# A hybrid backbone step: gates and half a modulation summed on VectorE from transposed weights, the state-space task run two groups at once, VectorE work moved to ScalarE

## The chip, the cores and the metric

The kernel runs on one core of a Trainium2 chip. The metric is the device time of one execution in microseconds (us), the median of three runs. The names of the trace are PE for TensorE's matmuls, PEld for its weight loads, DVE for VectorE, ACT for ScalarE, POOL for GpSimd and SP for the queue that issues most DMAs.

## The reference, cut to what matters

Two layers act on 384 tokens (128 context, 256 latent) of width 2048, all in float32.

```
mod = silu(c) @ w_ada + b_ada              # w_ada: 2048 x 6144; c for latent, c_ctx for context tokens
shift, scale, gate = split(mod, 3)         # 2048 columns each
u = LN(x) * (1 + scale) + shift
proj = u @ w_in                            # 2048 x 6160, feeds four mixers:
#   windowed attention, a state-space scan, pooling, neighbourhood attention
x = LN_affine(alpha * x + gate * (concat(silu(gate_g) * mixer_g) @ w_out))
```

So each layer needs two vectors (context, latent) times a 2048 x 6144 matrix, and two large products, u @ w_in and the mixers' output @ w_out.

## The kernel before, in words

The weights stream from DRAM once. A float32 weight tile of 128 x 1024 (`raw`) is split into a high part `whi` on ScalarE (`split_hi`, L1289) and the rest `wlo` on VectorE (`split_lo`, L1293), up to `HL_BUFS` = 4 items ahead of TensorE, and the activations are split likewise into `uhi` and `ulo`. Every product is three matmuls (`tok_mm` L1399, `t_mm` L1406). `CHUNKS` cuts the 6160 columns of w_in into 13 chunks; w_out follows in three groups of 512 columns (`cc` 0 to 2) and two of 256. Five PSUM banks take these products and are emptied by `evac` (L1018) and `wo_evac` (L1124); three serve all else (`mbank`).

The order on each engine is fixed when the program is built. `slots` (L1201 to L1250) lists the weight items; between two of them `advance` (L400) runs a step of a background task (attention units, convolutions, `gen_B`, `gen_Bs` and `gen_Bi` of the state space, pooling) where the clocks of `Plan` (L152) say that it is ready and that the work booked on VectorE and ScalarE ends at most `SLACK` us after TensorE's. `Plan` books a VectorE operation with two SBUF inputs and a GpSimd operation one after the other. `finish` forces tasks to their end where their results are needed; `finish_B` does so for the state space before the chunk `gd` is evacuated, because its output lies in the part of `mx` that `gd` writes.

The modulation (`ada_items` L1203) is computed on TensorE. A step is 512 columns of w_ada; its eight items, of two 128 x 512 weight tiles each, go in two bursts of four: `ada_mm` (L455) multiplies with the two vectors in four column strips of 32, `ada_evac` adds the strips up in `part`. For shift and scale `mod_mm` (L474) sums the four strips with `sel2` by four small matmuls and `mod_evac` adds the bias. For a gate (steps 8 to 11) `gen_gate` (L498) gathers the strips by one matmul with 512 columns, adds the bias, writes the row to DRAM (`gscr`) and reads it back on all 128 partitions. Layer 0's shift and scale are made at the start, beside its first three chunks. Layer 1's steps 0, 4, 1, 5, 2, 6 stand between layer 0's other chunks, its steps 3 and 7 in the layer boundary (`boundary`, L1416), and the gate steps of each layer in chunk `gc` and in cc 0 to 2.

`copy` (L337) alternates between ScalarE and VectorE where no engine is named. `unit` (L546) is one attention unit: scores, `tensor_tensor_reduce` for the maximum, exponential, and a scaling of the probabilities on VectorE.

Of the kernel before, what the change touches and what calls it, by code (L numbers as in the profile page):

```python
# [34 lines left out]
ARENA = 14600  # L35
# [3 lines left out]
HL_BUFS = 4  # L39

# [111 lines left out]
class Plan:  # L152
# [11 lines left out]
    def region(self, ap):  # L164
# [11 lines left out]
        if len(dims) > 1 and dims[0][1] <= 4:  # L176
# [6 lines left out]
              "arena", "bank")  # L183
# [25 lines left out]
    def cost(self, e, name, out, kw):  # L209
        src = kw.get("in_", kw.get("in0", out))  # L210
        n = max(math.prod(a.shape[1:]) for a in (out, src))
        if e == "PE":
            if name == "transpose":
                return 0.11
            wide = kw["rhs"].dtype == F32R
            c = 0.0105 + n * 0.00043 if wide else max(0.003 + n * 0.001675, 0.222)
            return c * 0.25 if kw.get("tile_position") is not None else c
        if e == "V":
            fast = name in ("tensor_copy", "tensor_scalar", "memset") and not src.tensor.name.startswith("bank")
            return 0.065 * (1 + hasattr(kw.get("scalar1"), "tensor")) + n * (0.00053 if fast else 0.00105)  # L220
        if e == "S":
            return 0.1 + n * 0.00083 + (0.18 if kw.get("accum_out") is not None else 0.0)
# [7 lines left out]
    def charge(self, e, name, args, kw):  # L230
# [3 lines left out]
               if hasattr(a, "tensor")]  # L234
        if e == "S" and args[2] in (AF.Exp, AF.Silu) and args[2] != self.table:
# [23 lines left out]
class Eng:  # L259
    def __init__(self, eng, key, plan):  # L260
        self.eng, self.key, self.plan = eng, key, plan

    def __getattr__(self, name):
        f = getattr(self.eng, name)

        def call(*a, **k):
            self.plan.charge(self.key, name, a, k)
# [5 lines left out]
def hybrid_step(ctx: ExitStack, tc: tile.TileContext,  # L273
                x_prompt, x_sample, cache_attn_k, cache_attn_v, cache_na_k, cache_na_v,
                state_f, state_b, c, c_ctx, w_ada, b_ada, w_in, w_out, ln_g, ln_b,
# [22 lines left out]
    bT = sb.tile([P, DEPTH, 2, KT], F32, name="bT")  # L298
# [19 lines left out]
    gscr = [dr.tile([4, 2, 512], F32, name=f"gscr{i}") for i in range(DEPTH)]  # L318
# [48 lines left out]
    WINDOW = 6  # L367
    BLOCKED = object()
    SLACK = 1.0
# [85 lines left out]
    def ada_mm(its):  # L455
        half = its[0]["i"] // 4
        bk = mbank()
        for g in range(2):
            for j in range(4):
                r = its[2 * g + j // 2]["raw"]  # L460
                PE.matmul(bk[32 * j:32 * j + 32, :], lhsT=scT[:, 8 * half + 4 * g + j, :],
                          rhs=r[:, (j % 2) * 512:(j % 2) * 512 + 512], start=g == 0, stop=g == 1,
# [3 lines left out]
    def ada_evac(its, bk):  # L466
        half = its[0]["i"] // 4
        if half == 0:
# [3 lines left out]
        return half == 1  # L472

    def mod_mm():  # L474
        bk = mbank()
        for b in range(4):
            PE.matmul(bk[:, 2 * b:2 * b + 2], lhsT=part[:, b * 128:b * 128 + 128], rhs=sel2, start=True, stop=True)
        return bk

    def mod_evac(l, step, bk):  # L480
# [4 lines left out]
        V.tensor_tensor(out=mod[:, l, w:w + nw, k:k + nk, :],  # L485
# [1322 lines left out]
```

## Time and profile before

| | us |
|---|---|
| median of 3 runs (1396.72 to 1399.25) | 1397.04 |
| the profiled execution, its own time | 1397.24 |
| its span, first to last instruction | 1395.5 |
| TensorE busy in it | 1342.4 |
| VectorE / ScalarE / GpSimd busy | 752.8 / 461.4 / 175.9 |

The span is the time between the first and the last instruction of the one execution that was profiled. Busy time is a union: two matmul records that overlap count once, and the end of a matmul is modelled. Start times in the trace are microseconds from the span's start.

### The profile page before, as it was taken

What the parts mean: (1) busy time and instruction counts of PE and PEld (TensorE: products, weight loads), DVE (VectorE), ACT (ScalarE), POOL (GpSimd) and SP (SyncE); (2) the same over time, 40 slices, a digit from 0 to 9 for tenths busy, and PEclk for the clock granted to TensorE, in tenths of its full rate; (3) what the DMA queues carried; (4) which work ended last, traced back from release to release, by engine and by line L of the source; (5) the groups of instructions that cost most, each with busy time, mean ns of one, the idle gap of its engine ahead of it and who ended that gap; (6) DMA issues with size and microseconds to landing.
All of it is one profiled execution on the core that took longest, in us unless ns stands there. A gap on an engine that the chain in (4) does not pass through costs nothing.

```text
span 1395.5 us, 19994 instructions
## 1 busy us (share of the span) xinstructions
PE 1342.4 (96%) x7769; PEld 1148.2 (82%) x7769; DVE 752.8 (54%) x1262; ACT 461.4 (33%) x709; POOL 175.9 (13%) x290
## 2 busy tenths in 40 slices
PE   5999999999999999999988999999999999999995
PEld 2776798899987999867786689999999899977785
DVE  4444555676574445554467344566456544554447
ACT  1222343332323243422228524333322343242220
POOL 1111110003430114000000000000234011300000
PEclk9999999999999999999998999999999999999998
DMA  9999764457675733777867544334555654577772
GB/s 328 357 357 301 243 190 152 139 167 260 206 252 185 247 103 109 258 249 244 274 201 248 174 134 118 91 110 120 146 150 166 170 154 115 163 246 258 265 233 96
DMA packets 179446, 278.29 MB, mean 199 GB/s; under 512 B 19688, under 2 KB 78968, under 8 KB 178456
## 3 DMA queue, kind: packets, MB, share of 16 engines
q1 hardware_dynamic: 176248, 269.07, 59.9%
q0 software_dynamic: 2240, 6.38, 1.6%
q10 hardware_dynamic: 864, 1.57, 0.3%
q8 instruction: 61, 1.00, 0.3%
q14 instruction: 33, 0.27, 0.1%
HBM read 267.98 MB, written 10.83 MB: 200 GB/s over the span
## 4 chain that ended last, share of the span: by engine, by line
PE 80%; DVE 6%; DMA 6%; issue 4%; ACT 3%; POOL 0%; SPq 0%; DVEq 0%; ACTq 0%; POOLq 0%
PE bank L268 80%; DVE arena L268 3%; DVE mx L268 2%; DMA rawa<-in_w_ada_dram 2%; DMA gscr<-arena 1%; ACT whi L268 1%; DVE wlo L268 1%; DMA arena<-gscr 1%; ACT arena L268 1%; DMA cst<-in_tables_dram 1%; DMA arena<-in_w_ada_dram 1%; ACT ucat L268 1%; DMA raw<-in_w_in_dram 0%; ACT uhi L268 0%; ACT L268 0%
## 5 line engine op out<-in xcount | busy, mean ns | idle before, releaser
L268 DVE TENSOR_TENSOR wlo<-raw,whi 128x1024 fp32r<-128x1024 f32 (+1 forms) x248 | 318.9, 1290 | 316.8 <-ACT whi L268 313.1
L268 ACT ACTIVATE whi<-raw 128x1024 fp32r<-128x1024 f32 (+1 forms) x256 | 269.4, 1058 | 400.6 <-PE bank L268 280.9
L268 PE MATMUL bank<-uhi,whi 128*128 128x384 f32 x1024 | 368.5, 360 | 4.3 <-ACT mx L268 2.7
L268 PE MATMUL bank<-whi,uhi 128*128 128x512 f32 (+2 forms) x960 | 344.8, 359 | 5.5 <-ACT uhi L268 4.0
L268 PE MATMUL bank<-uhi,wlo 128*128 128x384 f32 x1024 | 344.8, 337 | 0.0
L268 PE MATMUL bank<-ulo,whi 128*128 128x384 f32 x1024 | 344.5, 336 | 0.0
L268 PE MATMUL bank<-wlo,uhi 128*128 128x512 f32 (+2 forms) x960 | 337.8, 352 | 1.9 <-POOL wlo L268 1.9
L268 PE MATMUL bank<-whi,ulo 128*128 128x512 f32 (+2 forms) x960 | 338.2, 352 | 0.2 <-DVE ulo L268 0.2
L268 PEld LDWEIGHTS bank<-whi,uhi 128*128 128x128 f32 x960 | 183.1, 191 | 57.1 <-issue 14.5
L268 PEld LDWEIGHTS bank<-uhi,whi 128*128 128x128 f32 x1024 | 192.7, 188 | 21.2 <-issue 5.9
L268 PEld LDWEIGHTS bank<-wlo,uhi 128*128 128x128 f32 x960 | 183.3, 191 | 25.6 <-POOL wlo L268 2.6
L268 PEld LDWEIGHTS bank<-whi,ulo 128*128 128x128 f32 x960 | 182.6, 190 | 26.1 <-DVE ulo L268 1.1
L268 PEld LDWEIGHTS bank<-ulo,whi 128*128 128x128 f32 x1024 | 192.9, 188 | 5.8
L268 PEld LDWEIGHTS bank<-uhi,wlo 128*128 128x128 f32 x1024 | 192.2, 188 | 0.0
L268 ACT ACTIVATE arena<-arena 128x384 f32<-128x384 f32 (+7 forms) x85 | 44.1, 523 | 207.9 <-DVE arena L268 206.8
L268 PE MATMUL bank<-arena 128*128 128x128 f32 (+3 forms) x440 | 88.0, 325 | 0.1
L268 PE MATMUL bank<-rawa,scT 128*32 128x512 f32 x608 | 77.9, 604 | 8.1 <-DMA rawa<-in_w_ada_dram 8.1
L268 POOL TENSOR_TENSOR arena<-arena 128x512 f32<-128x512 f32 (+4 forms) x60 | 70.3, 1188 | 67.0 <-DVE arena L268 57.6
L268 ACT ACTIVATE arena<-bank 128x384 f32<-128x384 f32 (+2 forms) x92 | 39.0, 439 | 85.3 <-PE bank L268 82.9
L268 PEld LDWEIGHTS bank<-arena 128*128 128x128 f32 x440 | 64.4, 190 | 1.3 <-DVE arena L268 0.3
L268 PE MATMUL bank<-cst,arena 128*128 128x128 f32 (+1 forms) x273 | 45.6, 278 | 14.7 <-ACT arena L268 6.6
L268 PEld LDWEIGHTS bank<-rawa,scT 128*32 128x32 f32 x608 | 17.4, 109 | 47.3 <-issue 41.0
(83 smaller groups left out, 849.4 us busy)
## 6 DMA issues: line engine op xcount, KB each, us to landing
raw<-in_w_in_dram SPq DMA_DIRECT2D x176, 512.0 KB
rawa<-in_w_ada_dram SPq DMA_DIRECT2D x128, 512.0 KB
raw<-in_w_out_dram SPq DMA_DIRECT2D x64, 512.0 KB
arena<-in_w_ada_dram SPq DMA_DIRECT2D x80, 256.0 KB
rawa<-in_w_ada_dram SPq DMA_DIRECT2D x48, 256.0 KB
raw<-in_w_in_dram SPq DMA_DIRECT2D x16, 528.0 KB
arena<-lscr POOLq DMA_DIRECT2D x24, 256.0 KB, 4.6
arena<-gscr SPq DMA_DIRECT2D x8, 512.0 KB
```

What stands on the lines that cost most here:

```text
L268: return f(*a, **k)
```

## The change

- The gates of both layers, and steps 0, 4, 1, 5 of layer 1's shift and scale, are no longer made on TensorE. The host hands w_ada transposed as well (`w_adat`: a column of w_ada lies along a row). A tile holds 128 columns of w_ada on the partitions and 1024 of its 2048 rows; VectorE multiplies it by `silu(c)`, which is replicated on all partitions in `scb` (1 MB per half of the rows, read from the small DRAM tensor `csc`), and sums along the row with `tensor_tensor_reduce`, once for the context and once for the latent vector. `vq` lists 96 such tiles: 32 for layer 0's gate, 32 for layer 1's half of shift and scale, 32 for layer 1's gate. They lie in the four `rawa` buffers, and while w_out of layer 0 runs in two buffers of the arena.
- The reductions are placed by the planner: `v_fill` after each group of matmuls where VectorE's clock is behind TensorE's and the tile has landed, `v_hole` before a VectorE operation that would wait 0.6 us or more, and `v_until` where results are needed.
- A gate is finished by one transpose and one DRAM round trip per layer instead of four.
- `mod_mm` transposes the strips, and VectorE adds them up (`tensor_reduce`) in `mod_evac`.
- `gen_Bi` waits for and computes the decay of two groups ahead of the matmuls; its output has its own buffer `bo` in the arena, `finish_B` is gone, and the three norms are tasks of their own.
- From VectorE to ScalarE: modulation in `u_prep`, scaling in `unit`, the first tap of `gen_conv`, and `copy` gives ScalarE three of four.
- In the boundary `xn` has half its size (its second half is written after four transposes read the first), and `ucat` has four slots instead of three. `SLACK` is 2.0. Layer 1's steps 2 and 6 move to layer 0's cc 1 and 2. Some of `Plan`'s costs are changed, and the scratch for GpSimd's DMA descriptors is given as 4096 bytes.

```diff
+RAW_V = 2
+V_STEPS = (0, 4, 1, 5)
...
+    gcol = sb.tile([P, 2, KT], F32, name="gcol")
+    vpart = sb.tile([P, 32, 2], F32, name="vpart")
+    scb = sb.tile([P, 2, 1024], F32, name="scb")
-    ucat = sb.tile([P, 2, T], F32, name="ucat")
+    ucat = sb.tile([P, 2, 512], F32, name="ucat")
...
-            flip[0] ^= 1
-            eng = "S" if flip[0] else "V"
+            flip[0] = (flip[0] + 1) % 4
+            eng = "V" if flip[0] == 0 else "S"
...
+    V_HOLE = 0.6
-    SLACK = 1.0
+    SLACK = 2.0
...
-        V.tensor_tensor(out=mod[:, l, w:w + nw, k:k + nk, :],
-                        in0=bk[:, 0:8].rearrange("p (w k v) -> p w k v", w=nw, k=nk),
+        m = vsum[:, :, :]
+        V.tensor_reduce(out=m, in_=bk.rearrange("p (b j v) -> p b v j", b=4, j=4)[:, :, 0:2, :],
+                        axis=mybir.AxisListType.X, op=OP.add)
+        V.tensor_tensor(out=mod[:, l, w:w + nw, k:k + nk, :], in0=m.rearrange("p (w k) v -> p w k v", w=nw),
...
-            PE.matmul(bk[:, 2 * b:2 * b + 2], lhsT=part[:, b * 128:b * 128 + 128], rhs=sel2, start=True, stop=True)
+            PE.transpose(bk[:, b * 128:b * 128 + 128], part[:, b * 128:b * 128 + 128], ident)
...
-    def gen_gate(l, step):
-        cc = step - 8
+    def gen_gate(l, cc):
+        if cc == 0:
+            gt = yield from get(128)
+            bk = mbank()
+            PE.transpose(bk[0:32, 0:128], gcol[:, :, :].rearrange("p v k -> p (v k)"), ident)
+            copy(gt.v()[0:32, :], bk[0:32, 0:128], "S")
+            dma(nc.sync, gscr[l].rearrange("v (k p) -> (v k) p", p=P), gt.v()[0:32, :])
+            yield
+            gt.free()
-        src = bass.AP(tensor=b_ada.tensor, offset=b_ada.offset + l * 6144 + step * 512, ap=[[0, 2], [1, 512]])
-        dma(nc.gpsimd, gb.v(512, 1024)[0:2, :], src)
-        bk = mbank()
-        PE.matmul(bk[0:2, :], lhsT=sel2, rhs=part[:, :], start=True, stop=True)
-        V.tensor_tensor(out=gb.v(0, 512)[0:2, :], in0=bk[0:2, :], in1=gb.v(512, 1024)[0:2, :], op=OP.add)
-        dma(nc.sync, gscr[l][cc], gb.v(0, 512)[0:2, :])
-        yield
-        src = bass.AP(tensor=gscr[l].tensor, offset=gscr[l].offset + cc * 1024, ap=[[0, P], [1, 1024]])
-        dma(nc.sync, gb.v(), src)
+        src = bass.AP(tensor=gscr[l].tensor, offset=gscr[l].offset + cc * 512, ap=[[0, P], [D, 2], [1, 512]])
+        dma(nc.sync, gb.m(2, 512), src)
+    vq = []
+    vq += [dict(l=0, w=2, kt=j, half=h) for h in (0, 1) for j in range(KT)]
+    vq += [dict(l=1, w=s_ // 4, kt=4 * (s_ % 4) + j, half=h) for h in (1, 0) for s_ in V_STEPS for j in range(4)]
+    vq += [dict(l=1, w=2, kt=j, half=h) for h in (0, 1) for j in range(KT)]
+    vload, vdone = [0], [0]
+    vseen = {}
+    vhalf = [None]
+    vring = [rawa, []]
+    def v_load():
+        ring = vring[0]
+        while vload[0] < min(vlimit[0], vdone[0] + len(ring)):
+            it = vq[vload[0]]
+            c0 = it["w"] * D + it["kt"] * P
+            it["raw"] = ring[vload[0] % len(ring)]
+            dma(nc.sync, it["raw"][:, :], w_adat[it["l"], c0:c0 + P, it["half"] * 1024:it["half"] * 1024 + 1024])
+            vload[0] += 1
...
+    def v_half(h):
+        if vhalf[0] != h:
+            vhalf[0] = h
+            dma(nc.sync, scb[:, :, :], bass.AP(tensor=csc.tensor, offset=csc.offset + h * 1024,
+                                               ap=[[0, P], [D, 2], [1, 1024]]))
+    def v_step(more=True):
+        it = vq[vdone[0]]
+        v = it.setdefault("v", 0)
+        v_half(it["half"])
+        key = (it["l"], it["w"], it["kt"])
+        first = it["half"] == vfirst[it["l"], it["w"]]
+        if first and v == 0:
+            vseen[key] = vdone[0] % 32
+        slot = vseen[key]
+        init = bT[:, it["l"], it["w"], it["kt"]:it["kt"] + 1] if first else vpart[:, slot, v:v + 1]
+        if first:
+            dst = vpart[:, slot, v:v + 1]
+        elif it["w"] == 2:
+            dst = gcol[:, v, it["kt"]:it["kt"] + 1]
+        else:
+            dst = modcol(it["l"], it["kt"], it["w"], v)
+        V.before = None
+        V.tensor_tensor_reduce(out=uflat[:, :] if v == 0 else it["raw"][:, :], in0=it["raw"][:, :], in1=scb[:, v, :],
+                               scale=1.0, scalar=init, op0=OP.mult, op1=OP.add, accum_out=dst)
+        V.before = v_hole
+        it["v"] = v + 1
+        if v == 1:
+            vdone[0] += 1
+            if more:
+                v_load()
+            if vdone[0] < len(vq):
+                v_half(vq[vdone[0]]["half"])
+    def v_ready():
+        if vdone[0] >= vlimit[0] or vload[0] <= vdone[0]:
+            return 1e9
+        return max(plan.ready([], [vq[vdone[0]]["raw"], scb[:, :, :]]), clk["V"])
+    def v_hole(t):
+        while t - clk["V"] >= V_HOLE and v_ready() <= clk["V"] + 0.1:
+            v_step()
+    vlimit = [0]
+    vfirst = {(0, 2): 0, (1, 0): 1, (1, 1): 1, (1, 2): 0}
+    V_GATE = {0: 32, 1: 96}
+    V_ALL = {0: 64, 1: 96}
+    def v_until(n, more=True):
+        while vdone[0] < n:
+            v_step(more)
+    def v_fill():
+        while v_ready() <= clk["PE"]:
+            v_step()
...
-        u = ucat[:, kt % 2, :]
-        V.tensor_scalar(out=u[:, 0:128], in0=bk[:, 0:128], scalar1=modcol(l, kt, 1, 0),
-                        scalar2=modcol(l, kt, 0, 0), op0=OP.mult, op1=OP.add)
-        V.tensor_scalar(out=u[:, 128:384], in0=bk[:, 128:384], scalar1=modcol(l, kt, 1, 1),
-                        scalar2=modcol(l, kt, 0, 1), op0=OP.mult, op1=OP.add)
+        u = ucat[:, kt % 2, 0:T]
+        S.activation(u[:, 0:128], bk[:, 0:128], AF.Identity, bias=modcol(l, kt, 0, 0), scale=modcol(l, kt, 1, 0))
+        S.activation(u[:, 128:384], bk[:, 128:384], AF.Identity, bias=modcol(l, kt, 0, 1), scale=modcol(l, kt, 1, 1))
...
-        V.tensor_scalar(out=sc.v(0, nk), in0=sc.v(0, nk), scalar1=st[:, 2:3], scalar2=None, op0=OP.mult)
+        S.activation(sc.v(0, nk), sc.v(0, nk), AF.Copy, scale=st[:, 2:3])
...
-        V.tensor_scalar(out=o, in0=xp.v(0, 388), scalar1=w[0], scalar2=b, op0=OP.mult, op1=OP.add)
+        S.activation(o, xp.v(0, 388), AF.Identity, bias=b, scale=w[0])
...
-        return mx[:, 12 * T + 512 * t:12 * T + 512 * t + 512]
+        return lay[l]["bo"].v(512 * t, 512 * t + 512)
+        d["bo"] = yield from get(1536)
...
-        yield lr.v()
+        yield lr.v(0, 1024)
+        decay(0)
+        cb(1)
+        yield lr.v(1024, 2048)
+        decay(1)
+        yield
-            decay(i)
-            if i % 2 == 0 and t < 2:
-                cb(t + 1)
-            yield
+                if i == 1:
+                    cb(2)
+                yield lr.v(1024 * (i % 2), 1024 * (i % 2) + 1024)
+                decay(i + 2)
...
+        def norm(t):
+        for t in range(3):
+            spawn(norm(t), ("Bn", l, t), True)
...
-            if name == "gd":
-                finish_B(l)
...
-        o, x = lay[l]["xn"].v(2048 * t + c0, 2048 * t + c0 + n), mxX[:, t, c0:c0 + n]
+        o, x = lay[l]["xn"].v(1024 * t + c0 % 1024, 1024 * t + c0 % 1024 + n), mxX[:, t, c0:c0 + n]
...
-            for s in (0, 4, 1, 5, 2, 6):
+            for s in (2, 6):
-        gside = ada_items(l, 8)
-        for m in main:
-            slots.append(m)
-            if CHUNKS[m["ch"]][0] == "gc":
-                slots.append(gside.pop(0))
-            elif side and (CHUNKS[m["ch"]][2] == 512 or m["p"] % 2):
-                slots.append(side.pop(0))
+        slots += main
+        for cc in range(4):
+            for i, o in enumerate(o_items(l, cc)):
+                slots.append(o)
+                if side and cc in (1, 2):
+                    slots.append(side.pop(0))
-        for cc in range(4):
-            gside = ada_items(l, 9 + cc) if cc < 3 else []
-            for o in o_items(l, cc):
-                slots.append(o)
-                if gside:
-                    slots.append(gside.pop(0))
...
+        it["late"] = i >= 64
+                    if it.get("late") and not vring[1] and vdone[0] < V_ALL[0]:
+                        continue
...
-        xn = d["xn"] = ar.alloc(6144)
+        V.before = None
+        xn = d["xn"] = ar.alloc(3072)
...
-                add(("A", t, h), e, c - 0.5 + 0.1 * h + (1.0 if h == 2 else 0.0), [("Rr", t) if e == "V" else ("Rb", t)], [],
+                free = [("Ua", t, p) for p in range(4)] if h == 2 else []
+                add(("A", t, h), e, c - 0.5 + 0.1 * h + (1.0 if h == 2 else 0.0),
+                    [("Rr", t) if e == "V" else ("Rb", t)] + free, [xv(t, c0, n)],
...
+            if it["n"] > n_start and vlimit[0] < V_ALL[l]:
+                vlimit[0] = V_ALL[l]
+                v_half(vq[vdone[0]]["half"])
+                v_load()
+                V.before = v_hole
...
+                v_fill()
...
+                if l == 0 and cc == 0:
+                    v_move(True)
+                if l == 0 and cc == 3:
+                    v_until(V_ALL[l])
+                    v_move(False)
+            if cc == 0 and p == 1:
+                v_until(V_GATE[l])
+                spawn(gen_gate(l, 0), ("gate", l, 0), True)
+            if cc < 3 and p == 4:
+                spawn(gen_gate(l, cc + 1), ("gate", l, cc + 1), True)
```

## Rows read from the trace of the kernel before

**Rows 1.** The page, busy time of each engine and granted clock by slice.

```profile
PE 1342.4 (96%) x7769; PEld 1148.2 (82%) x7769; DVE 752.8 (54%) x1262; ACT 461.4 (33%) x709; POOL 175.9 (13%) x290
...
PEclk9999999999999999999998999999999999999998
```

**Rows 2.** Stages: length; busy us of PE, PEld, DVE, ACT, POOL; clock, DMA, GB/s.

```profile
0.00:176.00 176.00, 155.59 (x839) 108.36 (x839) 85.09 (x145) 46.29 (x59) 21.77 (x16) 0.98 0.96 315
176.00:577.00 401.00, 397.87 (x2468) 359.39 (x2469) 225.94 (x394) 137.87 (x223) 74.06 (x129) 1.00 0.58 185
577.00:698.00 121.00, 120.54 (x585) 88.60 (x584) 59.34 (x82) 33.32 (x41) 1.52 (x3) 1.00 0.77 262
698.00:725.00 27.00, 27.00 (x222) 26.00 (x221) 15.47 (x29) 4.64 (x6) 1.53 (x1) 1.00 0.68 226
725.00:786.00 61.00, 49.73 (x256) 34.19 (x256) 37.70 (x79) 43.94 (x92) 3.80 (x5) 0.91 0.67 223
786.00:1231.00 445.00, 441.37 (x2586) 414.52 (x2586) 239.94 (x403) 158.45 (x248) 68.71 (x130) 1.00 0.47 136
1231.00:1364.00 133.00, 133.00 (x679) 100.03 (x678) 63.54 (x86) 35.80 (x43) 1.52 (x3) 1.00 0.74 253
1364.00:1395.50 31.50, 17.28 (x146) 17.07 (x144) 25.79 (x49) 1.06 (x1) 2.97 (x3) 0.85 0.27 100
```

**Rows 3.** TensorE timeline, one modulation burst; start, length.

```profile
312.96 1.92 PE L268 MATMUL bank<-rawa,scT 128*32 128x512 f32 x16
314.81 0.44 PE L268 MATMUL bank<-uhi,whi 128*128 128x384 f32 x1
315.09 0.34 PE L268 MATMUL bank<-ulo,whi 128*128 128x384 f32 x1
315.27 0.34 PE L268 MATMUL bank<-uhi,wlo 128*128 128x384 f32 x1
```

**Rows 4.** TensorE timeline, a gate step's last matmul and its successor.

```profile
580.20 1.02 PE L268 MATMUL bank<-part,cst 128*2 128x512 f32 x2
581.15 0.50 PE L268 MATMUL bank<-whi,uhi 128*128 128x512 f32 x1
```

**Rows 5.** Lines of TensorE by shape: the small matmuls of shift and scale.

```profile
L268 PE MATMUL bank<-cst,part 128*128 128x2 f32 x128 | 15.5, 243 | 2.6 <-DVE part L268 1.6 <-DVE arena L268 0.9
```

**Rows 6.** TensorE timeline at the boundary, before and after its longest gap.

```profile
725.40 0.28 PE L268 MATMUL bank<-wlo,uhi 128*128 128x256 f32 x1
725.52 0.28 PE L268 MATMUL bank<-whi,ulo 128*128 128x256 f32 x1
729.54 0.84 PE L268 MATMUL bank<-cst,arena 128*128 128x128 f32 x6 [3.74 <-DVE arena L268]
...
732.24 0.41 PE L268 MATMUL bank<-wlo,uhi 128*128 128x256 f32 x1
732.45 0.41 PE L268 MATMUL bank<-whi,ulo 128*128 128x256 f32 x1
```

**Rows 7.** VectorE timeline, a softmax reduction and its accumulator read.

```profile
856.48 0.61 DVE L268 CUSTOM_DVE_ANT_0 arena<-bank,cst,prm 128x384 f32<-128x384 f32 x1
857.02 0.08 DVE L268 DVE_READ_ACCUMULATOR2_ANT arena<- 128x1 f32 x1
```

**Rows 8.** VectorE and GpSimd timelines, splits with and without GpSimd.

```profile
358.24 2.02 DVE L268 TENSOR_TENSOR wlo<-raw,whi 128x1024 fp32r<-128x1024 f32 x1 [1.34 <-ACT whi L268]
362.93 1.23 DVE L268 TENSOR_TENSOR wlo<-raw,whi 128x1024 fp32r<-128x1024 f32 x1 [2.66 <-ACT whi L268]
...
354.78 7.75 POOL L268 TENSOR_TENSOR arena<-arena 128x512 f32<-128x512 f32 x6 [12.34 <-DVE arena L268]
```

**Rows 9.** Lines of VectorE by shape: softmax scaling, first tap, strip evacuation.

```profile
L268 DVE TENSOR_TENSOR part<-bank,part 128x512 f32<-128x512 f32 x24 | 16.5, 687 | 45.1 <-PE bank L268 45.1
...
L268 DVE TENSOR_SCALAR arena<-arena 128x384 f32<-128x384 f32 x32 | 13.7, 428 | 1.1
...
L268 DVE TENSOR_SCALAR arena<-arena,colp 128x388 f32<-128x388 f32 x16 | 7.6, 476 | 0.0
```

More of the change, by code (lines that the diff above doesn't have):

```diff
@@ L234, in charge, with starts @@
                if hasattr(a, "tensor")]
+        return out, outs, ins
+    def starts(self, e, name, args, kw):
+        out, outs, ins = self.operands(args, kw)
+        t = self.ready(outs, ins, e)
+        return max(t, self.port) if self.shares_port(e, ins) else t
+    def charge(self, e, name, args, kw):
+        out, outs, ins = self.operands(args, kw)
         if e == "S" and args[2] in (AF.Exp, AF.Silu) and args[2] != self.table:
@@ L259 @@
 class Eng:
+    before = None
     def __init__(self, eng, key, plan):
@@ L266, in call @@
         def call(*a, **k):
+            if self.before is not None:
+                self.before(self.plan.starts(self.key, name, a, k))
             self.plan.charge(self.key, name, a, k)
@@ L455, in ada_mm @@
     def ada_mm(its):
-        half = its[0]["i"] // 4
         bk = mbank()
[L458 to L462, printed above, removed]
+        for n, it in enumerate(its):
+            for k in range(2):
+                j = 2 * (n % 2) + k
+                PE.matmul(bk[32 * j:32 * j + 32, :], lhsT=scT[:, 2 * it["i"] + k, :],
+                          rhs=it["raw"][:, k * 512:k * 512 + 512], start=n < 2, stop=n >= len(its) - 2,
                           tile_position=(0, 32 * j))
@@ L466, in ada_evac @@
     def ada_evac(its, bk):
-        half = its[0]["i"] // 4
-        if half == 0:
+        if its[0]["i"] == 0:
             copy(part[:, :], bk[:, :], "S")
@@ L471, in ada_evac @@
             V.tensor_tensor(out=part[:, :], in0=bk[:, :], in1=part[:, :], op=OP.add)
-        return half == 1
+        return its[-1]["i"] == 7
     def mod_mm():
@@ L1644, in hybrid_step @@
             if len(burst) == 4:
-                while any(t.name[0] in ("gate", "mod") for t in bg):
-                    run(next(t for t in bg if t.name[0] in ("gate", "mod")))
-                if ada_evac(burst, ada_mm(burst)):
-                    if it["step"] >= 8:
-                        spawn(gen_gate(l, it["step"]), ("gate", l, it["step"] - 8), True)
-                    elif l == 1:
-                        spawn(gen_mod(1, it["step"]), ("mod", 1, it["step"]), True)
+                while any(t.name[0] == "mod" for t in bg):
+                    run(next(t for t in bg if t.name[0] == "mod"))
+                if ada_evac(burst, ada_mm(burst)) and l == 1:
+                    spawn(gen_mod(1, it["step"]), ("mod", 1, it["step"]), True)
                 for b in burst:
```

80 lines of the change are left out of this document (48 added, 32 removed).

## The prediction

> **What bounds the kernel now.** I read the page first. TensorE is busy 1342.4 of 1395.5 us and its granted clock stays at the upper level in nearly every slice; VectorE is busy 752.8 us, ScalarE 461.4 [rows 1]. A busy matmul need not be a bound one, because the records overlap, so I cut the span into the kernel's stages next: start-up (three chunks of layer 0 beside its shift and scale), ten more chunks of layer 0, its output columns 0 to 1535, its last 512 columns, the layer boundary, and layer 1 [rows 2]. The reader is to see that TensorE waits only at the ends of this list: 20.4 us of the first 176, 11.3 of the 61 at the boundary, 14.2 in the tail. In the ten chunks of layer 0 it is idle 3.1 of 401 us, in those of layer 1 3.6 of 445, in the output stages 0.5 of 121 and none of 133. So in these stages a microsecond of TensorE work that goes is a microsecond of the end, as long as nothing else takes the lead. In them VectorE is busy 48 to 56% and the DMA engines 47 to 77%. Start-up is different: there the DMA share is 0.96, so TensorE time saved there is not counted.
>
> The sum is made against the profiled execution's 1397.2 us (its span and 1.7 us around it); the median of the runs is 1397.04, the same to 0.02%.
>
> **What is taken off TensorE.** The modulation product runs in bursts of four weight tiles: 8 matmuls in four column strips, 16 records. A burst begins at 312.96 and the next matmul at 314.81: 1.85 us. The matmul behind it is followed 0.28 us later, where its like is followed after 0.18: about 0.1 more [rows 3]. So 1.95 us a burst. Of the 48 bursts, 8 made layer 0's gate, 8 layer 1's gate and 8 half of layer 1's shift and scale (steps 0, 4, 1, 5): 24 x 1.95 = 46.8 us, all in stages that TensorE bounds (the other two shift and scale steps move from the chunks into the output stage, which is one as well).
>
> A gate step also ends in a matmul that gathers the strips: 580.20 to 581.15, 0.95 us, and the same 0.1 behind it; 8 x 1.05 = 8.4 us [rows 4]. In its place stand two transposes of about 0.1 each in the whole kernel. A shift and scale step ends in four small matmuls, 8 records: 15.5 us over 16 steps, 0.97 each [rows 5]. Four go: 3.9 us. The 12 that stay become four transposes: six such transposes took 0.84 us from the first start to the last end [rows 6], so four are some 0.55, and each step saves 0.4. Eight of these 12 lie in start-up and two in the boundary, where I count nothing; two count, 0.8 us. Together 46.8 + 8.4 + 3.9 + 0.8 - 0.2 = 59.7 us, and 1397.2 - 59.7 = 1337.5 us if nothing new waits. About 40 of the 59.7 lie between 176 and 698 (16 bursts, 4 gate steps, 4 small steps and the two cheaper ones), some 20 in layer 1.
>
> **What VectorE takes over.** 96 tiles of 128 x 1024, two reductions each (context and latent): 64 of them in layer 0 (32 for its gate, 32 for layer 1's half), 32 in layer 1. No row shows this operation on 1024 elements with both inputs in SBUF. Bounds from the nearest rows: the same custom operation on 384 elements holds VectorE from 856.48 until its accumulator read at 857.02, and the read is 0.08 [rows 7]; that is 0.62 and the least. A two-input subtraction of 1024 elements, both in SBUF, takes 1.23 us; the same one took 2.02 where it met GpSimd [rows 8], the most. I take 1.23 + 0.08 = 1.3, since length sets it and GpSimd runs in a small part of the time. So 166 us of new work in layer 0 and 83 in layer 1.
>
> Gone from VectorE are the softmax scaling (13.7 us on 384 columns), the convolution's first tap (7.6) and half of the 24 removed strip evacuations (16.5 for the 24 that it had) [rows 9]; ScalarE takes the first two, and three of four undirected copies, and at 33% has room in every stage.
>
> The balance of layer 0, 176 to 698: 522 us less 40 leave 482. VectorE had 225.9 + 59.3 = 285.2 [rows 2]; less half of 13.7, half of 7.6 and 8 evacuations of 0.69 that makes 269, and with 166 it is 435 of 482, or 90%. In layer 1's chunks it is 240 + 83 less some 11, 312 of about 440. The new reductions are put by the planner into VectorE's idle time and hold at most one operation ahead of what follows, and the weight halves are split up to four items ahead of TensorE, so a single delay of 1.3 us is covered. At 90% the cover is thin: when VectorE runs late by more than the split-ahead, TensorE waits for `wlo`, and at chunk ends for a bank that VectorE still has to copy.
>
> How late it gets hangs on GpSimd. A split that took 1.23 us alone took 2.02 inside GpSimd's run of 7.75 us [rows 8]: the two did not run side by side. GpSimd is busy 75.6 us in this stretch [rows 2]. If all of it shuts VectorE out, the need is 435 + 75.6 = 511 of 482, 29 us too much; if none, nothing is lost. The planner's clocks book the two one after the other, so it does not count on overlap. I take 7 us here, a quarter of the 29, because a quarter or more of VectorE's instructions read a PSUM bank, successive ones overlap by some 0.08 us, and the last of the 64 tiles may run on into the output stage. In layer 1 I take 1 us, and 1.5 for the start of the first stretch, where a 1 MB broadcast and four 512 KB tiles are issued on SP's queue ahead of the next weights, while the DMA share is 0.58.
>
> The Trainium skill, SBUF — State Buffer, "Who interferes with whom", says that a VectorE instruction with two SBUF inputs and a GpSimd instruction that reads SBUF hold a port pair in turn, the second waiting for the whole of the first. It speaks against this change, whose every reduction has two SBUF inputs. The 2.02 us row agrees with it; by the rule taken strictly the stretch would come to the 29 us of the rival below, by the overlap that I assume to 7.
>
> **The rest of the change.** Splitting the state-space task's waits, running its three norms as separate tasks and no longer draining it before `gd` is evacuated take away a point at which the program forces work. I cost it at nothing: TensorE was not idle there (3.1 us in the whole stretch). The cover is the `gd` evacuation's distance from the `gc` evacuation, which waits for the pooling tasks and so for this one; if that is gone, `gc` waits instead. The smaller `xn` makes the third normalising step wait for four transposes; this sits on the boundary's chain, which VectorE and ScalarE hold, and a fourth `ucat` slot eases the same chain. I put both at nothing, within 4 us either way. The gate's DRAM round trip falls from eight to two. The four `scb` reloads stop only VectorE's new work.
>
> **A stall costs more than its length.** After the 3.74 us gap at the boundary a 256-column matmul's successor starts 0.21 us later, where steady state has 0.12 [rows 6], and that stage's granted clock is 0.91 [rows 2], so part of it ran at the lower of the two levels, 1.2 instead of 2.4 GHz. Several gaps of that size in layer 0 would add as much again; this belongs to the upper end.
>
> **Forecast:** 1337.5 + 7 + 1 + 1.5 = 1347 us.
>
> **The rivals.** *VectorE and GpSimd together bound layer 0.* All of GpSimd's time excludes VectorE and the 29 us are lost: 1337.5 + 29 = 1366.5, and up to 1372 with slow-clock stretches. For it: 90% load and the 2.02 row. Against it: the PSUM-reading share. Chance 0.25. *Slower: a reduction costs twice what I take.* From (482 + 60 - 269) / 128 = 2.13 us an operation layer 0's VectorE need alone eats the whole 60 us; at 2.4, twice a 1.2 us pass, it is 269 + 307 = 576, 94 over the 482, while layer 1's chunks still fit (240 - 11 + 64 x 2.4 = 383 of 440), so 1337.5 + 94 = 1431. For it: no row of a two-SBUF reduction of this length, and the 2.02 row comes near. Against: 0.54 us for 384 elements and 1.23 for a two-SBUF subtraction of 1024 are nearly one price per element. Chance 0.05. *No gain, since transfers set the pace.* The same weights still travel; if DMA were what feeds TensorE, time would stay near 1397. Against: 0.58 and 0.77 in the stages where the bursts lie, against 0.96 in start-up. Chance 0.03. *My forecast*, small waits only: 0.67.
>
> **How the numbers follow.** The likeliest case alone spans 1335 (no new wait, and a few of the present ones gone) to 1358. The range must leave out at most 2 in 10: it takes in the first rival's 1366.5, so 1335 to 1368. A change of 0.2%, 2.8 us, is about what this kernel's measurement can tell from none. Faster: 0.67 + 0.25 = 0.92; within 0.2%: the third rival, 0.03; slower: 0.05.
>
> **What would show it.** Right: 24 bursts instead of 48, no gathering matmuls of 512 columns; TensorE busy near 1285 us; custom reductions, 192 more, at about 1.2 to 1.3 us; VectorE near 88% between 176 and 660; TensorE's idle time grown by some 10 us, ended by `wlo` or a bank copied by VectorE. Wrong: reductions of 2 us or more; TensorE waits of several us each in layer 0, with a clock below 1.0; a longer boundary; `gc` waiting for the pooling tasks.

## The result and the profile after

The changed kernel takes 1357.07 us (median of 4 runs, 1355.26 to 1358.87) against 1397.22 us of the kernel before beside it; the ratio is 0.971, 95% interval 0.9692 to 0.9728. That is faster, by 40 us where 50 were forecast. The profiled execution took 1358.87 us. Of the version without forced rows, below, one of four executions took 2961.68 us and is left out of its median.

The page of the changed kernel, busy times and granted clock by slice:

```profile
PE 1285.0 (95%) x7291; PEld 1138.6 (84%) x7291; DVE 925.7 (68%) x1511; ACT 514.0 (38%) x822; POOL 190.9 (14%) x282
...
PEclk9999999999998999899999999999999999999998
```

Against [rows 1], TensorE is busy 57.4 us less, as worked out (1282.7 expected), but the span is only 38.4 us shorter: TensorE's idle time grew from 53.1 to 72.1 us. VectorE has 172.9 us more.

The stages, cut at the same points of the kernel as [rows 2]; the columns are the same:

```profile
0.00:173.70 173.70, 151.34 (x807) 105.23 (x807) 72.57 (x119) 60.66 (x93) 21.78 (x16) 0.97 0.88 308
173.70:553.90 380.20, 367.73 (x2195) 352.12 (x2196) 331.31 (x550) 154.69 (x260) 87.37 (x128) 0.99 0.68 210
553.90:674.20 120.30, 116.95 (x550) 90.46 (x549) 84.62 (x126) 33.71 (x42) 0.00 (x0) 0.97 0.75 264
674.20:701.20 27.00, 27.00 (x229) 27.00 (x228) 16.40 (x33) 6.46 (x8) 1.52 (x1) 1.00 0.65 229
701.20:756.00 54.80, 46.27 (x240) 30.48 (x240) 34.82 (x76) 41.57 (x93) 2.75 (x5) 0.94 0.63 221
756.00:1209.00 453.00, 441.99 (x2559) 418.16 (x2557) 301.19 (x485) 180.49 (x287) 74.54 (x129) 0.99 0.55 165
1209.00:1326.60 117.60, 117.60 (x586) 99.22 (x586) 59.03 (x79) 36.26 (x44) 0.00 (x0) 1.00 0.55 179
1326.60:1357.10 30.50, 16.13 (x136) 15.93 (x134) 25.78 (x49) 0.11 (x1) 2.96 (x3) 0.81 0.29 104
```

Layer 1's output stage took about all of its gain (133.0 to 117.6 us, still never idle). Start-up and the boundary gained 2.3 and 6.2 us that were not counted. The ten chunks of layer 0 went from 401.0 to 380.2 and TensorE, idle 3.1 us there before, is idle 12.5; the output stage of layer 0 (121.0 to 120.3) gained almost nothing, partly because two of layer 1's steps moved into it; layer 1's chunks got longer, 445.0 to 453.0, with 11.0 us idle instead of 3.6. These three are where the rest of the gain went.

TensorE's waits by what ended them (us in all, times, longest), and the new operation on VectorE by shape:

```profile
PE bank L285 <- DVE arena L285: 17.0, 10, 7.0
...
PE bank L285 <- DMA arena<-in_state_ssm_fwd_dram: 4.4, 1, 4.4
PE bank L285 <- DVE ulo L285: 3.3, 1, 3.3
PE bank L285 <- DVE wlo L285: 2.1, 2, 1.9
```

```profile
L285 DVE CUSTOM_DVE_ANT_0 rawa<-rawa,scb,bT 128x1024 f32<-128x1024 f32 x48 | 62.9, 1310 | 0.6 <-DVE arena L285 0.2
...
L285 DVE CUSTOM_DVE_ANT_0 rawa<-rawa,scb,vpart 128x1024 f32<-128x1024 f32 x41 | 55.1, 1343 | 0.3
...
L285 DVE DVE_READ_ACCUMULATOR2_ANT vpart<- 128x1 f32 x96 | 7.9, 82 | 0.0
```

By shape a reduction takes 1.28 to 1.34 us on average; the bounds were 0.62 and 2.02 [rows 7, 8]. The wait for `wlo` that was forecast is small; the new idle time is a few single waits, each of 2 to 7 us, for something else. Three of them:

*Inside `vd`.* TensorE and VectorE timelines:

```profile
414.76 1.89 PE L285 MATMUL bank<-mx,arena 128*128 128x64 f32 x16
423.67 1.97 PE L285 MATMUL bank<-mx,arena 128*128 128x64 f32 x8 [7.01 <-DVE arena L285]
...
426.50 0.52 PE L285 MATMUL bank<-uhi,whi 128*128 128x384 f32 x1
426.82 0.52 PE L285 MATMUL bank<-ulo,whi 128*128 128x384 f32 x1
```

```profile
416.14 1.83 DVE L285 CUSTOM_DVE_ANT_0 rawa<-rawa,scb,vpart 128x1024 f32<-128x1024 f32 x1
417.90 0.08 DVE L285 DVE_READ_ACCUMULATOR2_ANT gcol<- 128x1 f32 x1
417.90 3.91 DVE L285 TENSOR_TENSOR arena<-arena 128x512 f32<-128x512 f32 x3
421.72 1.28 DVE L285 CUSTOM_DVE_ANT_0 ucat<-rawa,scb,bT 128x1024 f32<-128x1024 f32 x1
422.93 0.08 DVE L285 DVE_READ_ACCUMULATOR2_ANT vpart<- 128x1 f32 x1
422.93 0.69 DVE L285 TENSOR_TENSOR arena<-arena 128x512 f32<-128x512 f32 x1
```

The state-space product at 423.67 waits for the decay. VectorE has no gap meanwhile, and two reductions stand ahead of and between the decay's steps (416.14 and 421.72), the first stretched to 1.83 us and three steps of the decay to 3.91 (2.01 for the same three at 409.50) beside three GpSimd operations that run from 415.85 for 4.68 us. Behind the wait a 384-column matmul follows the last after 0.32 us instead of 0.18.

*Around the start of cc 0.* VectorE, between the last product of `mx` and the splits of the activations:

```profile
563.64 1.28 DVE L285 CUSTOM_DVE_ANT_0 ucat<-rawa,scb,vpart 128x1024 f32<-128x1024 f32 x1
564.85 0.08 DVE L285 DVE_READ_ACCUMULATOR2_ANT mod<- 128x1 f32 x1
564.96 1.28 DVE L285 CUSTOM_DVE_ANT_0 rawa<-rawa,scb,vpart 128x1024 f32<-128x1024 f32 x1
566.17 0.08 DVE L285 DVE_READ_ACCUMULATOR2_ANT mod<- 128x1 f32 x1
566.17 1.02 DVE L285 TENSOR_TENSOR ulo<-mx,uhi 128x384 fp32r<-128x384 f32 x2
```

These are the last two of eight reductions in a row from 556.04 on: moving the tiles from `rawa` to the arena (`v_move(True)`) forces every tile that is loaded. TensorE waits 3.29 us for `ulo` from 563.49; another 3.34 from 549.39, when two reductions stood ahead of the evacuation of `gc` (0.99 us at this place in the run without reductions, below).

*In layer 1's `qd`.* TensorE, VectorE, GpSimd and SP's queue:

```profile
984.60 1.11 PE L285 MATMUL bank<-cst,arena 128*128 128x128 f32 x4 [4.42 <-DMA arena<-in_state_ssm_fwd_dram]
```

```profile
972.68 7.59 DVE L285 TENSOR_TENSOR wlo<-raw,whi 128x1024 fp32r<-128x1024 f32 x2 [0.58 <-ACT whi L285]
```

```profile
973.01 2.05 POOL L285 TENSOR_TENSOR arena<-mx,arena 128x512 f32<-128x512 f32 x2
975.02 3.04 POOL L285 TENSOR_TENSOR arena<-mx,prm 128x512 f32<-128x512 f32 x3
```

```profile
969.95 9.58 SPq L352 DMA_DIRECT2D raw<-in_w_in_dram  x2
979.59 0.46 SPq L352 DMA_DIRECT2D arena<-in_state_ssm_fwd_dram  x1
```

No reduction is near. Two splits of 1.23 us take 7.59 together, the first of them 6.46, through the whole of GpSimd's five operations; the weight load that refills the split's `raw` buffer stands on SP's queue until 979.5, and behind it, in the same queue, the load of the state that TensorE waits for.

### The profile page after: what moved, and what is told of

It is laid out like the page before. It is cut to its first block, busy times and chain, and to the rows that moved or that the text cites. A ratio compares the mean times of both kernels' runs of the same rounds, so it can differ in the third digit from the quotient of the medians.

```text
span 1357.1 us, 19293 instructions
## 1 busy us (share of the span) xinstructions
PE 1285.0 (95%) x7291; PEld 1138.6 (84%) x7291; DVE 925.7 (68%) x1511; ACT 514.0 (38%) x822; POOL 190.9 (14%) x282
## 4 chain that ended last, share of the span: by engine, by line
PE 48%; DVE 7%; issue 1%; ACT 1%; DMA 1%; POOL 0%; DVEq 0%; SPq 0%; ACTq 0%
PE bank L285 48%; DVE mx L285 3%; DVE arena L285 2%; DVE wlo L285 1%; ACT whi L285 1%; DMA arena<-in_cache_na_k_dram 0%; DMA arena<-in_state_ssm_fwd_dram 0%; DVE ucat L285 0%; ACT arena L285 0%; ACT ucat L285 0%; DVE rawa L285 0%; POOL arena L285 0%; DVE ulo L285 0%; DVE part L285 0%; ACT L285 0%
## 5 line engine op out<-in xcount | busy, mean ns | idle before, releaser
L285 DVE TENSOR_TENSOR wlo<-raw,whi 128x1024 fp32r<-128x1024 f32 (+1 forms) x248 | 324.7, 1315 | 238.1 <-ACT whi L285 231.2
L285 ACT ACTIVATE arena<-arena 128x384 f32<-128x384 f32 (+6 forms) x139 | 73.8, 536 | 225.5 <-DVE arena L285 224.8
L285 POOL TENSOR_TENSOR arena<-arena 128x512 f32<-128x512 f32 (+4 forms) x60 | 77.7, 1312 | 89.2 <-PE bank L285 46.8
L285 ACT ACTIVATE arena<-bank 128x384 f32<-128x384 f32 (+2 forms) x118 | 50.5, 446 | 89.5 <-PE bank L285 84.3
L285 POOL TENSOR_TENSOR arena<-arena,prm 128x1 f32<-128x1 f32 x18 | 15.8, 879 | 409.2 <-DVE arena L285 409.2
L285 PE MATMUL bank<-cst,arena 128*128 128x128 f32 (+2 forms) x297 | 49.9, 284 | 15.7 <-ACT arena L285 5.6
L285 DVE CUSTOM_DVE_ANT_0 rawa<-rawa,scb,bT 128x1024 f32<-128x1024 f32 x48 | 62.9, 1310 | 0.6 <-DVE arena L285 0.2
```

The costliest lines, as they stand in the source:

```text
L285: return f(*a, **k)
```

## The experiments

The prediction's theory, A: the TensorE work that goes is worth its 59.7 us, and what is missing was lost to VectorE's lateness. Its rival, B: the removed bursts gave less than worked out. For the lost time two further readings: *single meetings*, each with a cause of its own that can be taken away, or *one pool of lateness*, which only moves. Ratios are against the kernel before, timed beside each run.

**No reductions.** Both counts are zero; `gcol` and the shift and scale hold constants.

```diff
-    V_GATE = {0: 32, 1: 96}
-    V_ALL = {0: 64, 1: 96}
+    V_GATE = {0: 0, 1: 0}
+    V_ALL = {0: 0, 1: 0}
```

> Leaves out all 192 reductions, their tiles' loads and the copies of the conditioning vector; the sums are constants set at the start, everything else is the changed kernel. Theory A (the new TensorE waits come from VectorE running late under the reductions): all of them go and the saving of TensorE work stands alone, 1397.2 - 59.7 = 1337.5, so 1332 to 1341 us. Theory B (the waits come from the other parts: state-space order, work moved to ScalarE, smaller xn): 1350 us or more.

1334.13 us, ratio 0.9554 (0.954 to 0.9569): 62.5 us below the kernel before. A holds, B falls: the removed work gives about what was forecast, and the reductions cost 22.9 us of it. Their 96 loads are gone in this run too; that the cost is VectorE's and not the loads' rests on the changed kernel's waits, of which only two name a transfer between start-up and the end, the state and a cache, 4.7 us together. Measured in the profiled executions from the start of a chunk to the start of the next (as all such times below), layer 0's ten chunks and cc 0 to 2 take 472.4 us; in the kernel before they took 513.3, so 40.9 us went where the prediction put about 40. In the changed kernel they take 491.9: the reductions cost 19.5 us there. The state wait stays (4.3 us).

**No reductions in layer 1.** The 64 for its gate are left out.

> Leaves out the 64 reductions of layer 1's gate only (layer 1 uses layer 0's gate). In the changed kernel layer 1's thirteen chunks take 410 us, where 398 were expected. Theory A: they fall to 397 to 400 and the whole to about 1345. Theory B, or a chance meeting of VectorE and GpSimd that needs no reductions: they stay at 405 or more, the whole at 1353 to 1358.

1352.9 us, 0.9688 (0.9674 to 0.9703): 4 us. Measured from `ga` to `gc`, eleven chunks, layer 1 takes 406.2 instead of 409.9. Of its two 2 us waits the one of 2.35 goes and that of 2.03 falls to 1.38; the one in `qd` stays (50.5 us against 50.7). So most of what layer 1 lost is not the reductions'.

**No reductions during the inner state-space tasks.**

```diff
     def v_ready():
+        if any(t.name[0] in ("Bs", "Bi") for t in bg):
+            return 1e9
```

> No reduction is placed while the state-space tasks gen_Bs or gen_Bi run; all 192 are still made, later. In the changed kernel TensorE waits 7.0 us at 416.7 for the decay of this task and then runs 10 us at the lower clock, and 4.4 us at 980. Theory A, in the form that reductions in the midst of the state-space chain cost most: both waits go, 8 to 14 us less, 1343 to 1349. If the order of two groups at once is the cause: the waits stay, 1355 to 1360. If lateness is only moved: new waits of like size elsewhere, no gain.

1356.81 us, 0.9724 (0.9708 to 0.974): no change. `vd` falls from 47.0 to 38.4 us, its 7 us wait is gone, the ten chunks take 6.4 us less, and cc 0 rises from 40.2 to 47.6. VectorE's and TensorE's rows there:

```profile
560.93 1.28 DVE L285 CUSTOM_DVE_ANT_0 ucat<-rawa,scb,vpart 128x1024 f32<-128x1024 f32 x1 [7.49 <-DMA scb<-csc]
```

```profile
566.62 0.79 PE L285 MATMUL bank<-whi,ulo 128*128 128x512 f32 x1 [10.88 <-DVE ulo L285]
```

The held reductions are forced at cc 0, now with a reload of `scb` among them: VectorE stands 7.49 us for the DMA and TensorE 10.88 us behind VectorE. So the wait in `vd` goes with the reductions, but the time moved. The reload of `scb` is part of it: "the four `scb` reloads stop only VectorE's new work" held as long as no point of the program forced reductions behind one.

**No forced row at cc 0.** No tile is loaded ahead from `gc`'s third item until the output stage.

```diff
+            if l == 0 and name == "gc" and p == 2:
+                vlimit[0] = vload[0]
...
+                    vlimit[0] = V_ALL[0]
                     v_move(True)
```

> From the third item of layer 0's chunk gc no more tiles are loaded until the output stage begins, so that the move to two arena buffers finds none to be reduced at once. In the changed kernel eight reductions run back to back there (556 to 566) and TensorE waits 3.3 us at 563.5. If that forced run is what costs: the wait goes and the output stage is some 5 us shorter, 1351 to 1354. If it is lateness that shows up anyway: 1356 to 1358.

1351.55 us, 0.9685 (0.9664 to 0.9707): 5.5 us; the wait for `ulo` is gone and cc 0 takes 36.0 instead of 40.2; cc 2 rose by 1.9. Layer 0's ten chunks and cc 0 to 2 together took 3.8 us less. Here most of the time did not come back.

**The state loaded early.** The two loads are issued at the start of `gen_B`, ahead of its work, instead of at the start of the state step.

> The two loads of the scan's start state are issued when gen_B begins, some 10 us earlier, ahead of the weight load on SP's queue that waits for the split at 972.7. That split took 6.5 us with GpSimd's run of five products beside it, and TensorE waited 4.4 us at 980 for the state; the wait stands also in the run without any reduction. If the chain is GpSimd's run, the held split, SP's queue, the state load, TensorE: the wait goes, layer 1's chunk qd falls from 50.7 to 41 to 44 us, the whole to 1347 to 1351. If the state is not what TensorE really waits for, or the held split alone stops it: qd stays near 50, the whole 1355 to 1359.

1351.09 us, 0.9662 (0.9648 to 0.9676): 6 us; `qd` of layer 1 takes 43.4 instead of 50.7. The long split is still there:

```profile
972.40 7.59 DVE L285 TENSOR_TENSOR wlo<-raw,whi 128x1024 fp32r<-128x1024 f32 x2 [0.58 <-ACT whi L285]
```

So these 7.59 us on VectorE left TensorE no wait of 0.8 us or more in `qd` once no load that it needed stood behind the weight load on SP's queue.

**The inner state-space loop as before.** Decay one group at a time, without the two groups ahead.

> gen_Bi's loop as before the change (wait for both groups, then decay, product, reload in turn); its own output buffer and the separate norms stay. If two groups ahead is what makes the 7.0 us wait at 416.7 (the product stands where the planner believes the decay done): that wait goes, 1346 to 1352. If the new order helps under a loaded VectorE: more waits in the chunks qd to vd of layer 0, 1360 or more. If it matters little: 1355 to 1359.

1356.79 us, 0.9709 (0.9692 to 0.9726): no difference. The wait in `vd` is 4.25 us instead of 7.0, others make up for it.

**The four moves from VectorE to ScalarE undone.**

> The four moves from VectorE to ScalarE are undone: modulation in u_prep, softmax scaling, first tap and every second copy are VectorE's again, some 50 us more on it over the kernel, about half in layer 0. If VectorE's load is what the new waits follow: longer by 8 to 25 us, 1365 to 1382. If the waits come from single collisions whatever the load: within 4 us of 1357.

1351.51 us, 0.9667 (0.9653 to 0.9682): *faster* by 5.6 us, against what I expected. Layer 0 lost 1.2 us (493.1 against 491.9 with cc 0 to 2), no more than chance; layer 1's chunks gained 7.9, and `qd` takes 41.1 there. In it the split starts 0.57 us before GpSimd's run instead of 0.33, and is not held:

```profile
968.96 1.22 DVE L285 TENSOR_TENSOR wlo<-raw,whi 128x1024 fp32r<-128x1024 f32 x1 [0.58 <-ACT whi L285]
```

```profile
969.53 2.57 POOL L285 TENSOR_TENSOR arena<-mx,arena 128x512 f32<-128x512 f32 x2
972.06 4.03 POOL L285 TENSOR_TENSOR arena<-mx,prm 128x512 f32<-128x512 f32 x3
```

GpSimd's last operation there met the next split, at 973.28, which took 1.90 us.

**Four edits together.** The early state, the stop of loading, no reduction from `gc`'s seventh item until its evacuation nor during the groups of `gen_Bi`, and steps 2 and 6 finished at the boundary.

> Three remedies together: early state loads, no tiles loaded ahead of the move to the arena buffers (as in the fourth run) with no reduction in the last two items of chunk gc, and no reduction from the first coefficients to the last product of gen_Bi; layer 1's two remaining modulation tasks are finished ahead of the boundary. If each wait has its own cause: 1357 - 5.5 - 8 - 8 - 4, so 1331 to 1341. If put-off reductions only make the output stage late: 1345 to 1355.

1343.48 us, 0.9609 (0.9593 to 0.9625): the fastest complete version, 13.6 us below the changed kernel, and between the two readings. `vd` takes 38.1 us, `qd` of layer 1 43.4. Still there is a wait of 6.18 us at 551.28, since the few reductions forced at cc 0 again span a reload of `scb`, and cc 3 with the boundary takes 133.5 us instead of 130.7.

**No forced rows at all.** Loading stops at `gc`'s first item, the last tiles may run until the end of cc 3, and nothing is held in `gen_Bi`.

> All the work is done. Compared with the changed kernel: the state is loaded at the start of gen_B; no tile is loaded ahead from the start of gc until the output stage, and no reduction is placed from gc's seventh item until its products are evacuated; the last tiles are reduced by the end of cc 3 and not before its first item, so that no point of the program forces a row of reductions. In the inner state-space task they run as in the changed kernel. If the waits are single meetings, each with its own place, the savings add up: 6 (state) + 5.5 (gc and cc 0) off 1357 and some 3 of the boundary stage, so 1341 to 1346, with the 7 us wait inside vd still there (vd near 47). If VectorE's lateness is one pool that only moves from place to place, as with the hold, something else waits and the time stays at 1349 to 1354.

1347.08 us (three executions, 1346.74 to 1350.56), 0.965 (0.9628 to 0.9671). Between the two readings: `qd` (43.3) and cc 0 (33.6, the same as without reductions) gave what they should and `vd` stayed at 47.0, but cc 1 and cc 2 rose from 74.9 to 82.9 us. The longest of the new waits there (the next are 1.61 and 0.86):

```profile
634.55 0.66 PE L285 MATMUL bank<-cst,part 128*128 128x128 f32 x4 [2.75 <-DVE part L285]
```

**The same, and only the last groups of `gen_Bi` kept free.**

> As the run before, and beside it no reduction is placed from the third group of the inner state-space task until its end, so that some three are left over for the end of cc 3. If the 7 us wait inside vd comes from reductions that stand in front of the decay, vd falls from 47 to 38-41 us and the time by 4 to 8 us against the run before, 1335 to 1341. If the lateness moves, cc 3 or gc grows by as much and the time stays within 2 us of the run before.

1346.61 us, 0.9633 (0.9607 to 0.9659), the same as the run before. `vd` fell by 3.0 us only (44.0, its wait 4.0 instead of 7.0) and `gc` by 2.7, while `gd` and `pc` rose by 4.3. The time moved. And 4.0 us of the wait in `vd` need no reduction near it. VectorE made none between 408 and 421, and yet the decay's three steps lasted 4.41 us beside GpSimd's run (2.02 at 409.27, without it):

```profile
415.09 4.41 DVE L285 TENSOR_TENSOR arena<-arena 128x512 f32<-128x512 f32 x3
```

```profile
414.80 4.15 POOL L285 TENSOR_TENSOR arena<-arena 128x512 f32<-128x512 f32 x3 [5.91 <-PE bank L285]
```

With the reductions held through the whole task, in the third run and the run of four edits, this decay fell behind GpSimd's run, took 2.01 us, and TensorE did not wait. So two things meet in `vd`, reductions in front of the decay and GpSimd's run beside it. A third is the place of TensorE's product: without any reduction the decay met GpSimd too (3.95 us at 397.48), and no wait came of it.

**No forced rows, and the moves to ScalarE undone.**

> As the run before the last, with the four moves from VectorE to ScalarE undone (modulation, softmax scaling, first tap and half of the undirected copies on VectorE again), some 25 us more on VectorE in all. If the moves are worth something once the single meetings are gone, it is slower than that run by 2 to 6 us; if they buy nothing, and undoing them in the changed kernel was faster only because one meeting did not take place, the two are within 2 us.

1356.74 us, 0.9715 (0.9699 to 0.9732): 9.7 us slower than the same kernel with the moves. Layer 0's stretch grew by 6.0 us (497.1 against 491.1) and cc 3 with the boundary by 4.3; layer 1's chunks fell by 1.9. So the moves are worth something outside layer 1's chunks. That undoing them was faster in the changed kernel came from layer 1, where it happened to part the split from GpSimd's run, as it does here.

Layer 0's ten chunks (`x0` to `gc`) with cc 0 to 2, and layer 1's eleven (`ga` to `gc`), us in the profiled executions:

| | layer 0 | layer 1 |
|---|---|---|
| before | 513.3 | 402.0 |
| changed | 491.9 | 409.9 |
| no reductions | 472.4 | 405.2 |
| none in layer 1 | 489.4 | 406.2 |
| none during the inner tasks | 493.1 | 408.0 |
| no forced row at cc 0 | 488.1 | 410.0 |
| state loaded early | 491.0 | 402.4 |
| inner loop as before | 492.6 | 408.0 |
| moves undone | 493.1 | 402.0 |
| four edits | 486.2 | 402.8 |
| no forced rows | 491.1 | 403.9 |
| the same, last groups free | 488.1 | 402.4 |
| no forced rows, moves undone | 497.1 | 402.0 |

These are single executions: layer 0 is the same program in the changed kernel and in the run without layer 1's reductions, 491.9 and 489.4, so 2 to 3 us in this column can be chance. In layer 0 every complete version with the moves lies between 486 and 493: of 19.5 us of lateness the best order got back 5.7. There the pool is the better reading, argued from this spread rather than shown. In layer 1 one edit gave 7.5 at once, and stayed in every later run: a single meeting.

## Why the prediction held, and which terms were off

**TensorE's work: right, its total with some luck.** 24 bursts ran (384 records at 16 a burst [rows 3]), the 512-column gathering matmuls of [rows 4] are gone, the small ones of [rows 5] are now 48 transposes, four for each of 12 steps, and TensorE's busy time is 1285.0. The term was 59.7 us; the run without reductions gained 62.5, with 4.3 us of the state wait still in it. Where the term was counted it came in two places of three: layer 0's stretch gave 40.9 us against about 40, and layer 1's cc 0 to 2 gave 15.3 (115.2 to 99.9) where six bursts and four gathering matmuls make 15.9. Layer 1's chunks grew by 3.2 instead of shrinking by 3.9, and start-up, boundary and tail made up for it with 10.6 us that no term had. The transfers' rival and B are refuted.

**The price of a reduction: right.** 1.3 us was taken; 151 of the 192, those that meet no GpSimd operation, took 1.28, and all lie at 1.28 to 1.34 by shape. The rival at twice the price falls.

**VectorE's load: somewhat below the forecast.** It was 331.31 of 380.20 us, 87%, in the ten chunks. With cc 0 to 2, where 435 us were expected, 331.3 + 84.6 = 416 came, with all of layer 0's 128 reductions in them; of 500.5 us that is 83%, not 88. The copies given to ScalarE and some smaller steps had not been taken off in the sum. So the waits were longer than forecast at a lower load than forecast.

**New waits in layer 0: mis-sized.** This is the step that failed: 7 + 1.5 us were priced, and the run without reductions shows 12.9 us in the ten chunks and 6.6 in cc 0 to 2, 19.5 in all. "TensorE waits of several us each in layer 0, with a clock below 1.0" was one of the prediction's own signs of being wrong, and it came. Of the 1.5 for the start of the first stretch nothing shows: TensorE has no wait of 0.8 us there until 216. The prediction let lateness act through the split-ahead of `wlo`, which hardly waited (2.1 us in all, 1.9 of them in the boundary). It acted through chains in which a result of VectorE is used at once: the decay, the evacuation of `gc`, `ulo`. There no distance of four items covers a reduction that stands in front. In `vd` GpSimd's run beside the decay did about as much (4.0 of the 7.0 us stayed when the reductions near it were put off). And a term was missing: points of the program that force reductions (`v_until`, `v_move`) put up to eight of them, 10 us, in front of whatever comes next. "A stall costs more than its length" was named and given no size: the mean clock fell from 0.989 to 0.979 of the span, which is (0.021 x 1357.1) - (0.011 x 1395.5) = 13 us more of full-speed time lost to the lower level in these two executions, part of it while TensorE waited. (The changed kernel's other executions had 0.982 to 0.983.) The stretch behind the 7 us wait:

```profile
416.00:424.00 8.00, 0.98 (x8) 0.85 (x7) 7.97 (x11) 1.40 (x3) 4.45 (x3) 0.78 0.41 128
424.00:431.00 7.00, 7.00 (x26) 7.00 (x26) 6.47 (x11) 2.58 (x6) 0.94 (x1) 0.52 0.46 142
431.00:442.00 11.00, 11.00 (x65) 11.00 (x64) 8.95 (x16) 3.92 (x7) 3.63 (x6) 1.00 0.54 160
```

These are the columns of the stages: TensorE idle for 7 us, then busy throughout at a clock of 0.52 (nearly all at 1.2 instead of 2.4 GHz), and at 1.00 again from 431 on.

**GpSimd: the mechanism right, its size between the two cases.** Sorting the changed kernel's 192 reductions by whether a GpSimd row overlaps them by more than 0.05 us, 151 took 1.28 us on average and 41 took 1.43; of the full splits 202 took 1.23 and 46 took 1.71. In the ten chunks that is 28 x 0.18 + 22 x 0.49 = 16 us of VectorE's time, against 20 x 0.39 = 8 before: 8 us more, not the 29 of the rival. The Trainium skill, SBUF — State Buffer, "Who interferes with whom", has the second of the two wait for the whole of the first. The trace agrees that they take turns, and differs in the row of `qd`: the split at 972.68 began ahead of GpSimd's first operation and yet lasted through all five. The 2.02 us that the prediction took for the most was not the most in the trace of before, as the last section shows.

**Layer 1: mis-sized, mostly for another reason.** 1 us was priced and 11.8 were lost: its eleven chunks were to shrink by 3.9 (two gate bursts) and grew by 7.9 (402.0 to 409.9). The runs divide it: without layer 1's reductions the chunks take 406.2, 3.7 less; with the early state 402.4, 7.5 less; together 11.2 of the 11.8. The second part is no VectorE load at all. The changed placement let a split and GpSimd's five operations start within 0.33 us, and the prediction followed none of the DMAs behind the splits on SP's queue. In the kernel before the same split started 0.60 us ahead of GpSimd and took 1.23 us. The meeting came with the moves to ScalarE: it is there without any reduction (6.46 us from 948.43 on) and gone in both runs that undo the moves (1.22 and 1.23 us).

**What was costed at nothing.** The inner loop's order is indeed worth nothing (put back: 1356.79); the separate norms and the own buffer were not tried by themselves. The boundary, put at nothing within 4 us, gained 6.2 (its longest gap is 2.27 us where [rows 6] showed 3.74), and start-up 2.3. What gave these was not tried. They took back part of the waits that were too small in the sum: without them the time would be some 1366, inside the stated range, whose upper end was made for the first rival, but outside the 1335 to 1358 of the forecast's own case, which 1357 just meets. That the range held is in this part luck.

**What stays open.** Layer 0's 19.5 us of lateness move more than they go, but not by a rule that was found: cc 1 and cc 2 lost 8 us in the version without forced rows with 19 reductions in them (9 and 10), where the first hold had as many (10 and 9) at 37.1 and 37.9 us. How much of the 13 us at the lower clock is paid for by waits of this change alone was not separated either.

## What to carry to other kernels

Moving work from the bounding engine to one with room pays what is removed, less what it makes late; count not only the helper's share of the stage but each place where the bound engine uses its result at once, and every point at which the program forces a backlog. Before trusting a price for such lateness, run the kernel with the moved work left out: the difference is the price. A load that TensorE will need should not stand in a queue behind a transfer that waits for a buffer.

## What the hardware showed that was not expected

A VectorE split of 1.23 us that began 0.33 us before GpSimd's first of five operations was held until the last had ended: 6.46 us for it and 7.59 with the next, with 5.1 us of GpSimd work. With 0.57 us between the starts it took 1.22, and GpSimd's first two operations took 2.57 us instead of 2.05. The distance of the starts alone does not decide it: in layer 0 of the kernel with the moves undone a split that began at 320.91, 0.20 us ahead of the same five operations, took 1.21 us, and GpSimd's first two took 4.11. What decides which of the two is stretched was not tried by itself.

The kernel before had such a meeting too, in layer 0, and the prediction passed over it:

```profile
325.94 6.91 DVE L268 TENSOR_TENSOR wlo<-raw,whi 128x1024 fp32r<-128x1024 f32 x2 [1.74 <-ACT whi L268]
```

There it cost TensorE no wait: the state load had been issued at 322.54, ahead of the weight load that waited for the split. Where the state load stood behind, as in layer 1 of the changed kernel, it cost some 6 us.
